# All queries and keys of a latent-attention layer made one stage earlier, stored to DRAM and loaded back; the gate rows made one stage later

## The chip, the cores and the metric

The kernel runs on one core of one Trainium2 chip. A core has a matrix engine (PE, with its weight loads shown apart as PEld), a vector engine (DVE), a scalar engine (ACT), a general engine (POOL) and a queue engine (SP) that here only starts transfers. On-chip operands lie in a memory of 128 partitions; matrix products land in PSUM, eight banks of 128x512 floats. The metric is the device time in microseconds (us); what is compared is the median of several executions, and lower is better.

## The reference

One layer of a diffusion backbone over 1024 latent tokens (`NL`) and 128 context tokens, 1152 in all (`NT`), with D = 1024. What matters here is the attention branch and the gates:

```
h      = rms_norm(x) * (1 + scale) + shift          # shift, scale, gate from silu(cond) @ w_ada
u_f, z_f, cq, ckv, k_rope, z_a, g_f, g_a = split(h @ w_in)
q      = rms_norm(cq, q_norm_g) @ w_uq               # 8 heads x (64 + 32 rotary)
k, v   = split(rms_norm(ckv, kv_norm_g) @ w_ukv)     # 8 heads x 64 each, plus 32 shared rotary key columns
attn   = softmax((q k^T + q_r k_r^T) / sqrt(96)) v   # latent queries see context cache + latent keys
y_f    = (fourier_mix(u_f) * silu(z_f)) @ w_f_out
y_a    = (attn * silu(z_a)) @ w_a_out
y      = rms_norm(x + gate * ((sigmoid(g_f)*y_f + sigmoid(g_a)*y_a) @ w_out), final_norm_g)
```

All products are made at nearly fp32 accuracy: each operand is split into a high and a low part, and `mm3` issues three matmuls (high x high, high x low, low x high) for every product.

## The kernel before

The work runs through stages, each with its own PSUM pool. First the input is normalised, transposed and mixed; then pairs of 128-column blocks of the input projection are made (`pair`, until about 427 us). After that come three stages that the change touches.

**The Fourier output map** (about 427 to 497 us, the loop `for m in range(8)` at L1027). For each of eight 128-channel blocks m and three chunks c of 384 tokens, twelve matmuls (four k-blocks of `mm3`) make a chunk; DVE multiplies it with the gate path `gfl` (L1044), and the row block `mf` is stored to DRAM. At the head of each m the weights and `gfl` of m+1 are loaded (`load_half`, `load_gf`, queued on SP). Between the chunks other work is woven in: `low_tr` transposes the low-rank rows of ten token tiles and splits them into `cqh/cql` (query latent), `kvh/kvl` (key-value latent) and the rotary rows 64 to 127 of the key tiles `KB` (latents) and `KC` (context); `load_gate`, `ada_rows` and `gate_row` make the 2x1024 gate row at m = 1 to 4; `k_up` makes the keys of heads 0 and 1 at m = 5; `q_chunk` makes one query chunk (head 0, tokens 0 to 383) at m = 7; `value_map` makes the values, seven of ten tiles here or just behind.

**Attention** (about 497 to 777 us). Eight heads run one after another. The order of their steps is written out by hand in `HSEQ` (heads 0 to 6) and `LSEQ` (head 7): `s` is a score chunk (`mm3` into PSUM and a DVE minimum, L1099), `m` the minimum over chunks, `e` the exponential on ACT (L1110), `T` a transpose of probabilities on PE (L1131) with its split by ACT (L1132) and DVE (`lo_dve`, L109), `V` the product with the values (L1151, L1152). In the same order stand `L` (load the next head's query weights and, for odd heads, the next pair's key weights), `Q` (three per head: chunks 1 and 2 of this head's queries and chunk 0 of the next head's, `q_chunk`) and `K` (`k_up`, one matmul group for a pair of heads, its copy on ACT at L981 and its splits on POOL; in even heads only the second half's splits, `k_split`). `P` in head 7 loads ahead for the merge stage.

**The merge** (about 777 to 840 us). For each m, `merge_part` makes the attention output map, gates it, adds `mf` and splits the sum into `mh/ml`; `load_out` loads and splits a part of the last weight matrix. `merge_open(m)` starts the loads of m + `AHEAD` (3). The last stage reads the gate row from `gate_d`.

The tiles named `U(...)` all come out of one pool of 43 equal buffers (`NU`), H tiles out of another of four. A planner places the instructions on each engine's queue by their priority in program order and by its own estimate of when their inputs and a free buffer are there; an engine then works through its queue strictly in that order, and SP does so too with its transfers.

Of the kernel before, what the change touches and what calls it, by code (L numbers as in the profile page):

```python
# [59 lines left out]
VS = (3, 0, 0)  # L60


@with_exitstack
def kernel(ctx: ExitStack, tc: tile.TileContext, a: dict):
# [376 lines left out]
    def split_w(src, shape):  # L441
        raw = U(shape, F32, "wr")
        nc.sync.dma_start(raw, src)
        return split(raw)
# [7 lines left out]
    low_d = dram.tile([9, P, 448], F32, name="low_d")  # L452
# [54 lines left out]
    def low_out(c, pss):  # L507
# [8 lines left out]
        for j, ps in enumerate(pss):  # L516
            t = 3 * c + j
            row = H([P, 448], s="low")
            xk = ps[:, 384:416].rearrange("p (a b i) -> p a b i", a=2, b=2)
            if t < 8:  # L520
# [6 lines left out]
                for r in range(2):  # L527
                    dve.tensor_tensor(out=row[:, 384 + 32 * r : 416 + 32 * r], in0=t2.rearrange("p a b i -> p (a b i)"),
                                      in1=t1.rearrange("p a b i -> p (a b i)"), op=ALU.add)
            else:  # L530
                for r in range(2):
# [318 lines left out]
    def low_load(i):  # L850

        rows = U([P, 2, 448], s="low")
        for e in range(2):
# [3 lines left out]
            else:  # L857
                nc.sync.dma_start(row[:, 256:384], a["cache_ckv"])
                nc.sync.dma_start(row[:, 384:416], a["cache_krope"])
                nc.sync.dma_start(row[:, 416:448], a["cache_krope"])  # L860
# [26 lines left out]

    for i, (kind, dst, blk, m) in enumerate(PAIRS):
# [12 lines left out]

    gate_d = dram.tile([2, D], F32, name="gate_d")
    grow = [U([2, D], F32, "grow") for _ in range(2)]
    nc.sync.dma_start(grow[1], a["b_gate"].to_broadcast([2, D]))

    def load_gate(j):
        parts = []
        for q in range(4):
            w = U([P, 2, 512], s="wgate")
            nc.sync.dma_start(w, a["w_gate"][j, q])  # L910
            parts.append(w)
        return parts

    def gate_row(rows, j):
        ps = MM()
        pe.matmul(ps[0:2, :], sel, rows, start=True, stop=True)
        sl = slice(j * 512, (j + 1) * 512)
        dve.tensor_tensor(out=grow[0][:, sl], in0=ps[0:2, :], in1=grow[1][:, sl], op=ALU.add)
        if j == 1:
            nc.sync.dma_start(gate_d, grow[0])  # L920

# [11 lines left out]
    def put_kv(ckvn, krd, kv_h, kv_l, kb, sl, gain=True):  # L933
# [3 lines left out]
        pe.transpose(pt[0:64, 128:256], krd, ident)  # L937
# [5 lines left out]
        for h, l in kb:  # L943
            act.copy(h[64:128, sl], pt[0:64, 128:256])
            dve.tensor_tensor(out=l[64:128, sl], in0=pt[0:64, 128:256], in1=h[64:128, sl].bitcast(F32), op=ALU.subtract)

    def low_tr(t, row):
        sl = slice(t * P, (t + 1) * P)
        ckn, kd = row[:, 256:384], row[:, 384:448]
        if t == 9:  # L950
            put_kv(ckn, kd, kvh[:, 1024:1152], kvl[:, 1024:1152], KB, slice(1024, 1152), False)
            return
        if t < 8:
            put_kv(ckn, kd, kvh[:, sl], kvl[:, sl], KB, sl)
        else:
            put_kv(ckn, kd, kch, kcl, KC, slice(0, 128))
# [14 lines left out]
    def k_up(wk, c, kf):  # L971
# [5 lines left out]
        mm3(ps[:, 0:n], wk[:, 0, :], wk[:, 1, :], rh, rl, True, True)  # L977
        for e in range(2):
            x = H([64, CH], s="kf") if e == 0 else None
            x = x[:, 0:n] if e == 0 else (kf[0][:, sl] if c < 3 else kf[1])  # L980
            act.copy(x, ps[64 * e : 64 * e + 64, 0:n])  # L981
            if e == 0:
                k_split(0, c, x)

    def k_split(e, c, x):
        if c < 3:
            sl = slice(c * CH, (c + 1) * CH)
            kh, kl = KB[e][0][0:64, sl], KB[e][1][0:64, sl]
        else:
            kh, kl = KC[e][0][0:64, :], KC[e][1][0:64, :]  # L990
        hi_pool(kh, x)
# [517 lines left out]
```

## Time and profile before

| | |
|---|---|
| Median of 3 runs (lowest to highest) | 937.79 us (937.47 to 938.55) |
| The profiled execution's own time | 938.17 us |
| Its span in the trace | 936.4 us |
| Mean granted PE clock | 0.989 |
| HBM read and written | 81.74 MB and 32.83 MB |
| Chain that ended last, share of PE | 76% |

The span runs from the first to the last instruction of the trace; the profiled execution's time is 1.8 us longer. A matmul's record lasts until its result is written, while the next one starts before that, so that busy time on PE is not a count of work: the distance between the starts of two matmuls is what one costs when they follow each other without a gap. A weight load (PEld) runs under the matmul before it; where PEld sits idle, PE's queue waits.

### The profile page before, as it was taken

What the parts mean: (1) busy time and instruction counts of PE and PEld (TensorE: products, weight loads), DVE (VectorE), ACT (ScalarE), POOL (GpSimd) and SP (SyncE); (2) the same over time, 40 slices, a digit from 0 to 9 for tenths busy, and PEclk for the clock granted to TensorE, in tenths of its full rate; (3) what the DMA queues carried; (4) which work ended last, traced back from release to release, by engine and by line L of the source; (5) the groups of instructions that cost most, each with busy time, mean ns of one, the idle gap of its engine ahead of it and who ended that gap; (6) DMA issues with size and microseconds to landing.
All of it is one profiled execution on the core that took longest, in us unless ns stands there. A gap on an engine that the chain in (4) does not pass through costs nothing.

```text
span 936.4 us, 15839 instructions
## 1 busy us (share of the span) xinstructions
PE 892.8 (95%) x5814; PEld 841.9 (90%) x5814; DVE 629.2 (67%) x1276; ACT 422.9 (45%) x1149; POOL 411.9 (44%) x494
## 2 busy tenths in 40 slices
PE   4878999999999999999999999999999999999996
PEld 3667999899999999998899999999999989988885
DVE  3898466655545544658538889889889887784333
ACT  7555374411112211135128787787787782212111
POOL 1586313674444448942051263263263126763221
PEclk9889999999999999999999999999999999999999
DMA  9923645422222244278733000000000147342222
GB/s 365 361 89 120 229 144 188 155 97 96 97 97 96 97 146 146 97 280 295 268 139 135 7 7 4 7 7 4 7 7 2 62 182 280 107 157 90 91 92 88
DMA packets 35797, 115.59 MB, mean 123 GB/s; under 512 B 4484, under 2 KB 9348, under 8 KB 35720
## 3 DMA queue, kind: packets, MB, share of 16 engines
q1 hardware_dynamic: 31688, 105.94, 31.5%
q10 hardware_dynamic: 3168, 6.16, 1.8%
q0 software_dynamic: 864, 2.49, 0.8%
q8 instruction: 46, 0.75, 0.3%
q14 instruction: 31, 0.25, 0.1%
HBM read 81.74 MB, written 32.83 MB: 122 GB/s over the span
## 4 chain that ended last, share of the span: by engine, by line
PE 76%; POOL 4%; DVE 3%; DMA 1%; ACT 1%; issue 1%; DVEq 0%; SPq 0%; ACTq 0%; POOLq 0%
PE mm L122 21%; PE mm L126 20%; PE mm L125 20%; PE mm L1131 6%; PE mm L1152 4%; PE mm L1151 3%; POOL z L761 1%; POOL z L765 1%; DMA fz_d<-z 1%; DVE tl L109 1%; POOL wp L106 1%; DMA wr<-in_w_f_out 1%; POOL mfl L1295 1%; DVE hTl L109 0%; PE mm L1186 0%
## 5 line engine op out<-in xcount | busy, mean ns | idle before, releaser
L1099 DVE TENSOR_REDUCE s<-mm 128x1 f32<-128x384 f32 (+1 forms) x200 | 104.8, 540 | 15.6 <-PE mm L126 13.8
L109 DVE TENSOR_TENSOR tl<-mm,th 128x384 fp32r<-128x384 f32 (+1 forms) x216 | 102.9, 504 | 16.8 <-ACT th L1132 16.2
L1110 ACT ACTIVATE p<-mm,s 128x384 f32<-128x384 f32 x192 | 110.2, 588 | 7.3 <-DVE s L1104 7.1
L122 PE MATMUL mm<-hTh,wp 128*128 128x288 f32 x352 | 104.4, 297 | 0.0
L125 PE MATMUL mm<-hTl,wp 128*128 128x288 f32 x352 | 104.4, 297 | 0.0
L126 PE MATMUL mm<-hTh,wp 128*128 128x288 f32 x352 | 104.3, 297 | 0.0
L1132 ACT CAST th<-mm 128x384 fp32r<-128x384 f32 (+1 forms) x216 | 89.4, 461 | 25.6 <-PE mm L1131 22.7
L1131 PE MATMUL mm<-c,p 128*128 128x128 f32 x576 | 95.7, 274 | 1.9 <-ACT s L981 0.5
L1131 PEld LDWEIGHTS mm<-c,p 128*128 128x128 f32 x576 | 71.7, 140 | 9.0 <-DVE tl L109 1.8
L122 PE MATMUL mm<-th,wp 128*128 128x288 f32 x264 | 78.4, 297 | 1.3 <-ACT th L559 0.6
L125 PE MATMUL mm<-tl,wp 128*128 128x288 f32 x264 | 78.1, 296 | 1.5 <-DVE tl L109 1.5
L126 PE MATMUL mm<-th,wp 128*128 128x288 f32 x264 | 78.1, 296 | 0.0
L1152 PE MATMUL mm<-tl,v 128*128 128x384 f32 (+1 forms) x216 | 74.0, 346 | 0.2 <-DVE tl L109 0.2
L1151 PE MATMUL mm<-th,v 128*128 128x384 f32 (+1 forms) x216 | 73.2, 343 | 0.0
L122 PE MATMUL mm<-kh,q 128*128 128x384 f32 x192 | 70.7, 368 | 0.4 <-DVE tl L109 0.3
L122 PEld LDWEIGHTS mm<-hTh,wp 128*128 128x128 f32 x352 | 67.0, 190 | 0.3 <-ACT u L792 0.3
L125 PEld LDWEIGHTS mm<-hTl,wp 128*128 128x128 f32 x352 | 66.8, 190 | 0.0
L126 PEld LDWEIGHTS mm<-hTh,wp 128*128 128x128 f32 x352 | 66.8, 190 | 0.0
L125 PE MATMUL mm<-kl,q 128*128 128x384 f32 x192 | 64.7, 337 | 0.0
L126 PE MATMUL mm<-kh,q 128*128 128x384 f32 x192 | 64.0, 338 | 0.0
L106 POOL TENSOR_SCALAR q<-qf 128x384 fp32r<-128x384 f32 x24 | 12.3, 512 | 104.1 <-DVE qf L1004 65.4
L122 PE MATMUL mm<-hi,mh 128*128 128x512 f32 (+1 forms) x152 | 57.7, 383 | 0.0
(343 smaller groups left out, 2580.8 us busy)
## 6 DMA issues: line engine op xcount, KB each, us to landing
wr<-in_w_in SPq DMA_DIRECT2D x24, 512.0 KB, 4.2
x<-in_x_sample SPq DMA_DIRECT2D x16, 512.0 KB, 4.8
wada<-in_w_ada SPq DMA_DIRECT2D x16, 512.0 KB, 10.2
h_d<-hf SPq DMA_DIRECT2D x8, 576.0 KB, 3.3
gf_d<-z SPq DMA_DIRECT2D x8, 576.0 KB, 4.7
gfl<-gf_d SPq DMA_DIRECT2D x8, 576.0 KB, 4.6
mf_d<-mf SPq DMA_DIRECT2D x8, 576.0 KB, 3.2
gal<-ga_d SPq DMA_DIRECT2D x8, 576.0 KB, 3.7
```

What stands on the lines that cost most here:

```text
L106: pool.tensor_scalar(out=out, in0=x, scalar1=1.0, scalar2=1.0, op0=ALU.mult, op1=ALU.mult)
L109: dve.tensor_tensor(out=out, in0=x, in1=hi.bitcast(F32), op=ALU.subtract)
L122: i = pe.matmul(out, lh, rh, start=start, stop=False, skip_group_check=on)
L125: pe.matmul(out, lh, rl, start=False, stop=False, skip_group_check=on)
L126: pe.matmul(out, ll, rh, start=False, stop=stop, skip_group_check=on)
L761: pool.tensor_tensor(out=out, in0=out, in1=tmp, op=ALU.mult)
L1099: dve.tensor_reduce(out=self.nb if self.last else self.mx[:, kc : kc + 1], in_=ps[:, 0:n], axis=AX.X, op=ALU.min)
L1110: act.activation(self.p[:, kc * CH : kc * CH + n], self.ps[kc][:, 0:n], AF.Exp, scale=-1.0, bias=self.nb, accum_out=SSP[(self.h // 2) % 2] ...
L1131: pe.transpose(pt[:, j * P : (j + 1) * P], self.pr[j][:, kt * P : (kt + 1) * P], ident)
L1132: act.copy(th[:, i, 0:n], pt[:, 0:n])
L1151: pe.matmul(po[:, 0:n], V[kt][:, h, :], th[:, i, 0:n], start=(self.nv == 0), stop=False)
L1152: pe.matmul(po[:, 0:n], V[kt][:, h, :], tl[:, i, 0:n], start=False, stop=(self.nv == 8))
```

## The change

All 24 query chunks (8 heads x 3) and all 16 key groups (4 pairs of heads x 4 chunks) are made inside the Fourier output map, and each is stored to DRAM (`q_d`, `k_d`). A list `TASKS` says what stands behind each of the 24 chunks of that map (`L` low_tr, `W` and `w` weights, `k`, `q`, `v` value map, `K` the load of head 0's keys, `Q` the load of a query chunk of head 0). In attention, `L` becomes the load of the next head's keys into `KB`/`KC` (four transfers into partitions 0 to 63), `Q` the load of a query chunk one or two chunks ahead, and `K` does nothing. The orders `HSEQ` and `LSEQ` stay as they are. The high part of a query is copied by ACT instead of POOL; keys are split by ACT and DVE straight from PSUM for both heads of a pair at once. The rotary key columns are written four times instead of twice into a low-rank row (512 wide instead of 448), so that their transpose lands on partitions 64 to 127 by itself. The gate row's loads, matmuls and store move into the merge.

```diff
+TASKS = (
+    "L0 L1", "L2 L3 W", "L4 L5 W", "L6 L7", "L8 L9 W", "k00 k01", "k02 k03 q00", "q01 q02 W", "k10 k11 k12", "k13 q10 q11 W", "q12 q20",
+    "q21 q22", "k20 k21 k22", "k23 q30 q31", "q32 q40", "q41 q42", "k30 k31 k32 w", "k33 q50 q51", "q52 q60", "q61 q62", "q70 q71 K Q0",
+    "q72 v Q1", "v v", "v v", "v v",
+)
...
-            row = H([P, 448], s="low")
+            row = H([P, 512], s="low")
...
-                for r in range(2):
+                for r in range(4):
                     dve.tensor_tensor(out=row[:, 384 + 32 * r : 416 + 32 * r], in0=t2.rearrange("p a b i -> p (a b i)"),
...
+    def up_weights():
+        if not wk:
+            wk.extend(split_w(a["w_uk"].rearrange("h p c -> p h c"), [P, 4, P], lo_pool))
+        else:
+            p = len(wq)
+            wq.append(split_w(a["w_uq"][2 * p : 2 * p + 2].rearrange("h p c -> p h c"), [P, 2, 256], lo_pool))
...
+    q_d = dram.tile([NH, 3, P, 2, CH], F32, name="q_d")
+    k_d = dram.tile([4, P, 2, NT + P], F32, name="k_d")
...
-    def k_up(wk, c, kf):
+    def k_up(p, c):
...
-        mm3(ps[:, 0:n], wk[:, 0, :], wk[:, 1, :], rh, rl, True, True)
-        for e in range(2):
-            x = H([64, CH], s="kf") if e == 0 else None
-            x = x[:, 0:n] if e == 0 else (kf[0][:, sl] if c < 3 else kf[1])
-            act.copy(x, ps[64 * e : 64 * e + 64, 0:n])
-            if e == 0:
-                k_split(0, c, x)
...
+        mm3(ps[:, 0:n], wk[0][:, p, :], wk[1][:, p, :], rh, rl, True, True)
+        k = U([P, 2, CH], F32R, "k")
+        act.copy(k[:, 0, 0:n], ps[:, 0:n])
+        lo_dve(k[:, 1, 0:n], ps[:, 0:n], k[:, 0, 0:n])
+        nc.sync.dma_start(k_d[p][:, :, sl], k.bitcast(F32)[:, :, 0:n])
+
+    def k_load(h):
+        rows = slice(64 * (h % 2), 64 * (h % 2) + 64)
+        src = k_d[h // 2][rows]
+        for (kh, kl), sl in ((KB[h % 2], slice(0, NT)), (KC[h % 2], slice(NT, NT + P))):
+            nc.sync.dma_start(kh[0:64, :].bitcast(F32), src[:, 0, sl])
+            nc.sync.dma_start(kl[0:64, :].bitcast(F32), src[:, 1, sl])
+
+    def q_up(h, c):
...
         q = U([P, 2, CH], F32R, "q")
-        hi_pool(q[:, 0, :], qf)
+        act.copy(q[:, 0, :], qf)
         lo_pool(q[:, 1, :], qf, q[:, 0, :])
-        return q
+        nc.sync.dma_start(q_d[h, c], q.bitcast(F32))
+
+    def q_load(h, c):
+        t = U([P, 2, CH], F32R, "qt")
+        nc.sync.dma_start(t.bitcast(F32), q_d[h, c])
+        return t
...
     for m in range(8):
-        if m in (1, 3):
-            wgt = load_gate(m // 2)
-        elif m in (2, 4):
-            rows = ada_rows(wgt, 2, 512, MM())
...
+            for k in TASKS[3 * m + c].split():
+                task(k)
...
             elif o == "L":
                 if h + 1 < NH:
-                    if h % 2:
-                        wk, kf = load_split(a["w_uk"][h // 2 + 1], P), new_kf()
-                    wq1 = load_split(a["w_uq"][h + 1], 256)
+                    k_load(h + 1)
...
             elif o == "Q":
                 nq += 1
-                if nq < 3:
-                    qs[nq] = q_chunk(wq, nq)
+                if nq == 1:
+                    qs[2] = q_load(h, 2)
                 elif h + 1 < NH:
-                    q0 = q_chunk(wq1, 0)
+                    qn[nq - 2] = q_load(h + 1, nq - 2)
...
+    wgt, rows = [load_gate(0), load_gate(1)], []
     merge_open(0)
     merge_open(1)
...
     for m in range(2, 8):
         merge_open(m)
+        if m > 2 and rows:
+            gate_row(rows.pop(0), m - 3)
+        if wgt:
+            rows.append(ada_rows(wgt.pop(0), 2, 512, MM()))
         for c in range(3):
             merge_part(m, c)
```

More of the change, by code (lines that the diff above doesn't have):

```diff
@@ L450, in load_r @@
         return t
-    low_d = dram.tile([9, P, 448], F32, name="low_d")
+    low_d = dram.tile([9, P, 512], F32, name="low_d")
     f_d = dram.tile([4, P, NT], F32, name="f_d")
@@ L530, in low_out @@
             else:
-                for r in range(2):
+                for r in range(4):
                     act.copy(row[:, 384 + 32 * r : 416 + 32 * r], ps[:, 384:416])
@@ L850, in low_load @@
     def low_load(i):
-        rows = U([P, 2, 448], s="low")
+        rows = U([P, 2, 512], s="low")
         for e in range(2):
@@ L858, in low_load @@
                 nc.sync.dma_start(row[:, 256:384], a["cache_ckv"])
-                nc.sync.dma_start(row[:, 384:416], a["cache_krope"])
-                nc.sync.dma_start(row[:, 416:448], a["cache_krope"])
+                for r in range(4):
+                    nc.sync.dma_start(row[:, 384 + 32 * r : 416 + 32 * r], a["cache_krope"])
         return rows
@@ L898 @@
         pair(b, nb_, kind, dst, m, fs, {} if nb_ else {0: fz_load, 1: low_loads, 7: gf_first, 5: fz_split})
[L902 to L920, printed above, removed]
     cqh = [U([P, NT], F32R, "cqh") for _ in range(2)]
@@ L943, in put_kv @@
         for h, l in kb:
-            act.copy(h[64:128, sl], pt[0:64, 128:256])
-            dve.tensor_tensor(out=l[64:128, sl], in0=pt[0:64, 128:256], in1=h[64:128, sl].bitcast(F32), op=ALU.subtract)
+            act.copy(h[64:128, sl], pt[64:128, 128:256])
+            lo_dve(l[64:128, sl], pt[64:128, 128:256], h[64:128, sl])
     def low_tr(t, row):
         sl = slice(t * P, (t + 1) * P)
-        ckn, kd = row[:, 256:384], row[:, 384:448]
+        ckn, kd = row[:, 256:384], row[:, 384:512]
+        if t == 8:
+            put_kv(ckn, kd, kch, kcl, KC, slice(0, 128))
+        else:
+            ks = sl if t < 8 else slice(1024, 1152)
+            put_kv(ckn, kd, kvh[:, ks], kvl[:, ks], KB, ks, t < 8)
         if t == 9:
-            put_kv(ckn, kd, kvh[:, 1024:1152], kvl[:, 1024:1152], KB, slice(1024, 1152), False)
             return
[L953 to L956, printed above, removed]
         pt = MM()
@@ L1068 @@
         za.append(z)
-    for _ in range(3):
-        value_map(len(V))
+    for k in TASKS[24].split():
+        task(k)
     stage.close()
@@ L1220 @@
             osb = U([P, NT], F32, "osb")
-        nk = nq = npre = 0
-        q0 = None
+        nq = npre = 0
+        qn = {}
         for part in LSEQ if h == NH - 1 else HSEQ:
@@ L1297, in merge_part, with load_gate, gate_row @@
         lo_dve(ml[m][:, sl], mf[:, sl], mh[m][:, sl])
+    gate_d = dram.tile([2, D], F32, name="gate_d")
+    grow = [U([2, D], F32, "grow") for _ in range(2)]
+    nc.sync.dma_start(grow[1], a["b_gate"].to_broadcast([2, D]))
+    def load_gate(j):
+        parts = []
+        for q in range(4):
+            w = U([P, 2, 512], s="wgate")
+            nc.sync.dma_start(w, a["w_gate"][j, q])
+            parts.append(w)
+        return parts
+    def gate_row(rows, j):
+        ps = MM()
+        pe.matmul(ps[0:2, :], sel, rows, start=True, stop=True)
+        sl = slice(j * 512, (j + 1) * 512)
+        dve.tensor_tensor(out=grow[0][:, sl], in0=ps[0:2, :], in1=grow[1][:, sl], op=ALU.add)
+        if j == 1:
+            nc.sync.dma_start(gate_d, grow[0])
     def merge_open(m):
```

76 lines of the change are left out of this document (28 added, 48 removed).

## The prediction

> **What bounds the kernel now.** I read the page's first part, then the busy times of chosen stretches (columns: stretch, length, then busy us with the number of instructions for PE, PEld, DVE, ACT, POOL; granted clock; DMA share; GB/s).
>
> ```profile
> span 936.4 us, 15839 instructions
> PE 892.8 (95%) x5814; PEld 841.9 (90%) x5814; DVE 629.2 (67%) x1276; ACT 422.9 (45%) x1149; POOL 411.9 (44%) x494
> 427.00:496.50 69.50, 69.08 (x394) 61.13 (x393) 41.32 (x94) 24.59 (x70) 18.86 (x28) 1.00 0.64 233
> 496.50:566.60 70.10, 69.77 (x457) 67.39 (x456) 60.05 (x144) 55.78 (x171) 27.25 (x45) 1.00 0.09 32
> 566.60:636.60 70.00, 69.69 (x468) 67.36 (x467) 60.40 (x147) 55.34 (x173) 29.40 (x50) 1.00 0.02 6
> 636.60:706.60 70.00, 69.69 (x467) 67.36 (x466) 60.40 (x147) 55.26 (x172) 29.38 (x50) 1.00 0.02 6
> 706.60:777.00 70.40, 67.75 (x458) 64.08 (x457) 62.28 (x153) 54.29 (x166) 18.29 (x33) 1.00 0.30 104
> 777.00:840.00 63.00, 62.18 (x339) 59.73 (x339) 51.27 (x62) 12.25 (x24) 45.45 (x40) 1.00 0.51 172
> ```
>
> The first stretch is the Fourier output map, the next four are the pairs of heads, the last is the merge. PE bounds all three stages: it is busy over 98% of each but the last pair of heads (96%), at full clock. Busy matmuls overlap, so I check the pace by the starts of matmuls that follow without a gap. From the order of time on PE, the first and the last of 40 matmuls of 384 columns in a row, and three pieces of the chain that ended last:
>
> ```profile
> 165.68 0.34 PE L126 MATMUL mm<-hTh,lo 128*128 128x384 f32 x1
> ...
> 172.54 0.34 PE L126 MATMUL mm<-hTh,lo 128*128 128x384 f32 x1
> 457.83 1.85 PE mm L231 x16
> 464.10 0.95 PE mm L916 x2
> 508.20 0.66 PE mm L1131 x6
> ```
>
> 39 steps in 6.86 us: 0.176 us for each 384-column matmul. A 128-column one costs 0.66/6 = 0.11. So PE has work without a gap almost everywhere, and moving PE work from one stage to another gains nothing by itself: only places where PE waits can be won, and any new wait is paid in full.
>
> **The change part by part.** *Moved PE work.* A query chunk is 2 x 3 matmuls of 384 columns, 6 x 0.176 = 1.06 us. 23 of 24 chunks leave attention (one is made in the map already). A pair's keys are 9 such matmuls and 3 of 128 columns, 1.58 + 0.33 = 1.9 us; three of four pairs leave. Attention loses 23 x 1.06 + 3 x 1.9 = 30.1 us of PE work, the map gains 30.1. The gate's two groups of 16 matmuls and two of 2 (rows above: 1.85 and 0.95) are 2 x (1.85 + 0.95) = 5.6 us that leave the map and are added to the merge. Sum over the stages: 0. The transposes of rotary keys get wider weights, but stay 128-column matmuls: 0.
>
> *Waits that go.* In attention PE waits once per pair, where the pair's keys are made:
>
> ```profile
> 626.60:631.60 5.00, 4.69 (x30) 3.82 (x29) 3.43 (x9) 4.97 (x16) 5.00 (x9) 1.00 0.10 30
> PEld mm L1131 <- ACT s L981: 1.2, 3, 0.4
> 556.27 0.26 ACT L981 COPY kf<-mm 64x128 f32<-64x128 f32 x1 [1.91 <-PE mm L126]
> ```
>
> ACT stands 1.91 us at the copy of the last key chunk, since that copy is ahead of the probability splits on its queue; PE then waits for those. In the second pair's five microseconds weight loads are idle 5.00 - 3.82 = 1.18 us, and the row of the waits says three times. I take 3 x 1.2 = 3.6 us as gone. What is late next there is DVE (below). In the map, PE waits for the gate's transfers and for weights queued on SP behind them:
>
> ```profile
> PEld mm L122 <- POOL whl L106: 1.3, 1, 1.3
> PEld mm L231 <- DMA wgate<-in_w_gate: 0.9, 2, 0.6
> 436.82 5.44 DMA wr<-in_w_f_out
> ```
>
> 1.3 + 0.9 = 2.2 us gone. Together -5.8 us.
>
> *DVE in attention, the cover that shrinks.* Rows of DVE and ACT, the query's and key's own work, and two stretches inside the second pair of heads:
>
> ```profile
> L1004 DVE TENSOR_TENSOR qf<-mm,tab 128x384 f32<-128x384 f32 x24 | 13.2, 552 | 2.1 <-PE mm L126 1.2 <-PE mm L1131 0.4 <-issue 0.3
> L981 ACT COPY kf<-mm 64x384 f32<-64x384 f32 x24 | 11.4, 477 | 13.3 <-PE mm L126 13.0
> L112 POOL TENSOR_TENSOR q<-qf,q 128x384 fp32r<-128x384 f32 x24 | 24.3, 1013 | 1.5
> 576.60:581.60 5.00, 5.00 (x37) 4.91 (x36) 5.00 (x13) 4.33 (x13) 1.90 (x3) 1.00 0.04 13
> 606.60:611.60 5.00, 5.00 (x35) 4.89 (x35) 5.00 (x14) 4.61 (x15) 2.48 (x6) 1.00 0.02 3
> ```
>
> Of PE a pair loses 6 x 1.06 + 1.9 + the wait of 1.2 = 9.5 of 70.0 us; DVE loses only 6 x 0.552 = 3.3 of 60.4 (the key splits are on POOL). So PE would need 60.5 us, DVE 57.1: its share rises from 86% to 94%. ACT loses 6 x 0.477 and some, to 52 of 60.5. Already now DVE has stretches of five microseconds without a gap. Bounds: below, 0, since PE keeps its pace in just those two rows; above, DVE holds no higher share than its present 60.40/70.00, a pair then lasts 57.1/0.863 = 66.2, that is 5.7 more for each of four pairs, 23 us. The nearest rows are the two stretches, near the low end; I take one new DVE wait per pair of the size of the ACT wait that it replaces, 4 x 1.2 = +4.8 us. POOL's query splits (24 x 1.01 us) leave attention, but PE waits for POOL nowhere there: 0.
>
> *The map: transfers, buffers, SP's order.* Stores of 24 x 0.393 MB of queries and 5.24 MB of keys are added here. While they are made (from `k00` to `q72` of the task list: 17 chunks x 12 matmuls x 0.176 = 35.9, 24 query chunks 25.4, four key pairs 7.6; 68.9 us), the stage also stores six `mf` and loads five `gfl` (11 x 0.59 MB), five `w_f_out` blocks, two query weights and the value weight (8 x 0.262 MB), and for attention one set of keys and one query chunk (1.05 MB): in all 24.3 MB, 353 GB/s. The page has the rate of each 23.4 us slice:
>
> ```profile
> GB/s 365 361 89 120 229 144 188 155 97 96 97 97 96 97 146 146 97 280 295 268 139 135 7 7 4 7 7 4 7 7 2 62 182 280 107 157 90 91 92 88
> ```
>
> At its best, 365, the 24.3 MB take 66.6 of 68.9 us: hidden, but with 3% to spare. The Trainium skill ("DMA: Bandwidth & Descriptors", section Where 436 GB/s comes from) puts the limit between HBM and one core at about 358 GB/s, which speaks against this change; an estimate by that page is 67.9 us, 1.3 more, still under PE's time. The first slice's 365 lies above the page's figure, so the measurement decides.
>
> New waits: SP's store of a query waits for POOL's low part (1.01 us) behind ACT's copy, and behind it on SP stand the next m's weights and `gfl`; ACT's copy into the query tile waits for one of 43 buffers, and the splits of keys and values stand behind it on ACT. Counted from the code, 36 buffers are taken at m = 3 (8 fz, 4 cq, 2 kv, 4 key tiles, tab, 10 weights, 7 of the map itself), which leaves 7 for tiles on their way out. Bounds: 0, since loads run one m (12 us) ahead; above, the wait for `whl` of 1.3 us in each of six m, 8 us. I take two of them, +2.6 us. Elsewhere the map has cover: ACT 24.59 and DVE 41.32 of 69.50, and 40 copies of 0.477 and 40 DVE operations of 0.552 come into a stage that grows by 22 us net.
>
> *Merge.* 4.2 MB of gate weights are loaded while 43 buffers are short (attention's own end holds many, and the row from SP's order of time shows loads of `w_out` that wait already):
>
> ```profile
> 807.15 23.66 SPq L443 DMA_DIRECT2D wr<-in_w_out x4
> wgate<-in_w_gate SPq DMA_DIRECT2D x8, 512.0 KB, 5.7
> ```
>
> Freed in turn are the query and key latents and the table (7 buffers), so head 7's loads can start sooner. Bounds 0 to 4.4 (the gate's waits as in the map, 2.2, for each of its two halves); I take 1.
>
> *Low rows.* 16 more DVE operations and two on ACT:
>
> ```profile
> L528 DVE TENSOR_TENSOR low<-s,s 128x32 f32<-128x32 f32 x16 | 3.3, 246 | 0.2
> low<-low_d SPq DMA_DIRECT2D x9, 224.0 KB, 7.1
> ```
>
> 16 x 0.246 = 3.9 us at most on a DVE with gaps there, and 0.3 MB more to store and load. If that cover is gone, the last tiles' four operations cost 1 us; I take 0.3.
>
> *Key and query loads in attention.* 0.66 MB and three query chunks a head, against 6 GB/s now, issued a third of a head or more ahead: 0. No row shows a transfer into 64 partitions; at twice the time per byte it would still be hidden.
>
> *Sum*, against the profiled execution's own 938.17 (span 936.4 and 1.8 around it): -5.8 + 4.8 + 2.6 + 1.0 + 0.3 = +2.9, 941.1; the median of the runs lies 0.4 lower, so **940.7**.
>
> **The rivals.** *PE alone stays the bound (faster).* Place: attention. All waits that go are won and DVE follows at 94%; then 937.8 - 5.8 + 1 to 3 of small change = 933 to 935. For it: PE's pace in the two stretches with a DVE without a gap. Against it: the hand-written order was laid out with `Q` and `K` in it, each of which gave DVE about half a microsecond to catch up. It decides from there on that DVE's new waits stay under 3.9 us in all.
>
> *A wash.* DVE and the map cost about half of what I take: 936 to 939.6.
>
> *The map becomes bound by transfers and buffers.* Loads stand behind stores at 97% of the best rate, and PE waits in most m: the 8 us of the upper bound instead of 2.6, or a rate that holds only at 297 to 339 GB/s, as in this stage's stretches now:
>
> ```profile
> 420.00:425.00 5.00, 5.00 (x38) 5.00 (x37) 5.00 (x9) 2.56 (x7) 2.61 (x3) 1.00 0.94 339
> 440.00:465.00 25.00, 24.57 (x143) 19.00 (x137) 15.50 (x39) 7.26 (x23) 2.69 (x5) 1.00 0.80 297
> ```
>
> 24.3 MB at 339 are 71.7 us (+2.2), at 297 81.8 (+12.3): 943 to 953. Against it: at 0.80 share the second row isn't full.
>
> *It doesn't do what it says*: attention doesn't get shorter, because DVE bounds it at its present share: the upper bound above, up to 959. A full DVE beside a full PE speaks against it.
>
> **How the numbers follow.** Forecast (DVE and queues give back more than is won, 939.7 to 944): 0.36. PE alone: 0.27. Wash: 0.24. Transfers or DVE bound (944 to 959): 0.13. The range 932.8 to 948.5 leaves out little below (all waits won and more) and the upper part of the last case. A measurement here tells about 0.2% (1.9 us) from no change; faster 0.27, within it 0.24, slower 0.49.
>
> **What would show it.** Attention ends about 250 us after it starts, now 280; the map lasts about 92, now 69.5; the merge about 69, now 63. In the waits of attention, "ACT s L981" is gone, and weight loads wait for DVE's splits and PSUM instead, in four places or more. In the map, DMA share is over 0.9 and POOL's `whl` waits for its load. I am wrong if attention's PE is idle less than 4 us more than its work (then faster), or if PE waits over 5 us in the map (then 945 and up).

## The result and the profile after

The changed kernel takes **953.12 us** (median of 4 runs, 951.75 to 954.83) against 937.63 for the kernel before in the same measurement (4 runs, 936.87 to 938.55): a ratio of 1.0166, 95% interval 1.0146 to 1.0185, so 15.5 us slower. The forecast was 940.7 with a range of 932.8 to 948.5: the direction was right, the size was not.

The page of the profiled execution (952.68 us), first part: PE's busy time is 4.0 us longer than before, POOL's 56.5 us shorter, and the span is 14.2 us longer. So the 14 us are mostly time in which PE has nothing to do.

```profile
span 950.6 us, 16026 instructions
PE 896.8 (94%) x5814; PEld 838.1 (88%) x5814; DVE 635.3 (67%) x1307; ACT 426.5 (45%) x1159; POOL 355.4 (37%) x393
GB/s 365 363 75 137 224 168 227 74 115 120 119 103 111 128 67 125 162 315 194 329 377 370 68 53 78 78 9 71 78 79 20 136 162 340 171 149 101 89 89 89
```

Where it came from is read from PE's matmuls in order of time: the last matmul of the pair loop (`acc` pairs, the front's end), the first score, and the first matmul of the merge. "Forecast" is the sum of the prediction's terms for that stretch.

| stretch | before, us | after, us | change | forecast |
| --- | --- | --- | --- | --- |
| start to the end of the pair loop | 424.1 | 418.0 | -6.1 | +0.3 (low rows) |
| from there to the first score (map) | 71.9 | 101.1 | +29.2 | +24.9 (30.1 - 5.6 - 2.2 + 2.6) |
| first score to the merge (attention) | 280.7 | 264.2 | -16.5 | -28.9 (-30.1 - 3.6 + 4.8) |
| merge and output, to the end | 159.7 | 167.3 | +7.6 | +6.6 (5.6 + 1.0) |
| span | 936.4 | 950.6 | +14.2 | +2.9 |

Attention is short of the forecast by 12.4 us, the map by 4.3, the merge by 1.0; the front gave back 6.4 that nobody had counted. The stages as busy times of chosen stretches, after (columns as above: stretch, length, then busy us with instructions for PE, PEld, DVE, ACT, POOL; granted clock; DMA share; GB/s): the map, the four pairs of heads, the merge, and attention as a whole.

```profile
418.00:519.00 101.00, 97.05 (x547) 93.75 (x546) 63.62 (x134) 38.32 (x100) 43.57 (x46) 0.98 0.89 311
519.00:584.00 65.00, 61.92 (x400) 57.72 (x398) 55.17 (x135) 51.08 (x157) 3.20 (x8) 1.00 0.29 96
584.00:649.00 65.00, 62.82 (x417) 58.96 (x417) 56.69 (x141) 51.81 (x162) 7.07 (x15) 1.00 0.20 58
649.00:714.00 65.00, 62.81 (x417) 58.95 (x417) 56.81 (x141) 51.81 (x162) 7.08 (x15) 1.00 0.20 58
714.00:783.30 69.30, 65.60 (x436) 59.80 (x437) 59.91 (x148) 55.02 (x169) 10.03 (x21) 1.00 0.30 104
783.30:841.50 58.20, 56.72 (x328) 51.60 (x327) 42.94 (x57) 11.21 (x22) 37.80 (x35) 1.00 0.61 226
519.10:783.30 264.20, 253.05 (x1669) 235.37 (x1668) 228.59 (x562) 209.62 (x650) 27.38 (x59) 1.00 0.25 79
```

Attention of the kernel before, in the same view:

```profile
496.00:776.70 280.70, 277.10 (x1843) 266.35 (x1841) 243.32 (x589) 221.06 (x675) 104.02 (x175) 1.00 0.11 37
```

Two things are to be seen. DVE was busy 243.32 of 280.70 us before, 86.7%, and is busy 228.59 of 264.20 after, 86.5%: its share has not risen at all. And PE has 174 matmuls fewer, while weight loads, whose busy time overlaps least, are idle 28.8 us instead of 14.4. A pair in the middle has lost 50 matmuls of its 467 and only 5.0 us of its 70.0; the matmuls alone are 8.3 (6 x 1.06 + 1.9).

The waits of weight loads in attention (us in total, times, longest). The one row for the keys, "ACT s L981", is gone as forecast. In its place stand many short waits, more of them for ACT's probabilities and sums (L1105; 11.6 us in all rows of the view) than for DVE (6.3 us). The four largest:

```profile
PEld mm L1146 <- ACT s L1105: 3.6, 7, 0.7
PEld mm L1126 <- DVE osb L1160: 3.2, 5, 0.9
PEld mm L1126 <- ACT p L1105: 2.8, 9, 0.8
PEld mm L129 <- ACT p L1105: 2.3, 2, 1.9
```

The groups of the page show the ring behind them. Each row ends with the engine's idle time ahead of it and what ended it: DVE's minimum waits for PE's scores, ACT's exponential for DVE's minimum (L1099 after, L1104 before), DVE's split of the transposed probabilities for ACT's copy (L1127 after, L1132 before). First before, then after:

```profile
L1099 DVE TENSOR_REDUCE s<-mm 128x1 f32<-128x384 f32 (+1 forms) x200 | 104.8, 540 | 15.6 <-PE mm L126 13.8
L1110 ACT ACTIVATE p<-mm,s 128x384 f32<-128x384 f32 x192 | 110.2, 588 | 7.3 <-DVE s L1104 7.1
L109 DVE TENSOR_TENSOR tl<-mm,th 128x384 fp32r<-128x384 f32 (+1 forms) x216 | 102.9, 504 | 16.8 <-ACT th L1132 16.2
L1094 DVE TENSOR_REDUCE s<-mm 128x1 f32<-128x384 f32 (+1 forms) x200 | 105.2, 541 | 19.6 <-PE mm L133 17.8
L1105 ACT ACTIVATE p<-mm,s 128x384 f32<-128x384 f32 x192 | 110.2, 592 | 9.3 <-DVE s L1099 9.2
L116 DVE TENSOR_TENSOR tl<-mm,th 128x384 fp32r<-128x384 f32 (+1 forms) x216 | 101.9, 504 | 12.2 <-ACT th L1127 11.3
```

The engines waited for each other in this way before the change too, and for about as long (39.7 us in the three rows, 41.1 after). New is that PE, with less work of its own, now waits for the ring. The chain that ended last, taken from the first score to the merge, before and after (the view cuts its line off at the end):

```profile
by line: PE mm L1131 21.5%; PE mm L122 16.2%; PE mm L126 15.7%; PE mm L125 15.5%; PE mm L1152 11.8%; PE mm L1151 11.5%; DVE tl L109 1.5%; PE mm L1186 1.4%; ACT th L1132 0.9%; DVE s L1099 0.9%; ACT p L1110 0.6%; issue 0.5%; DVE osb L1165 0.4
by line: PE mm L1126 16.3%; PE mm L1146 11.9%; ACT p L1105 10.8%; PE mm L1147 9.8%; PE mm L129 9.5%; PE mm L133 8.9%; PE mm L132 8.9%; DVE tl L116 4.9%; DVE s L1094 4.8%; ACT th L1127 4.7%; issue 2.6%; DVE osb L1160 1.2%; ACT s L1105 1.1%;
```

Before, ACT and DVE hold some 4% of that chain, after some 27%: the path through attention now runs through both.

The map after its start, and the start itself:

```profile
430.00:515.00 85.00, 84.45 (x486) 82.81 (x486) 49.96 (x103) 29.01 (x73) 38.63 (x41) 1.00 0.92 323
423.00:426.40 3.40, 1.18 (x7) 0.46 (x5) 3.21 (x9) 1.85 (x7) 0.17 (x1) 0.99 0.99 344
426.50:429.70 3.20, 2.87 (x9) 2.90 (x10) 3.04 (x12) 2.96 (x12) 1.47 (x2) 0.50 0.11 32
```

From 430 to 515 PE is busy 84.45 of 85.00 us with the DMA share at 0.92: the transfers are hidden. The loss is at the start. The task list packs ten low-row transposes (`L0` to `L9`) into five chunks, their copies and splits pile up on DVE (busy 3.21 of 3.40 us) and PE waits; then the granted clock is 0.50 for 3.2 us. The two waits there:

```profile
PEld mm L957 <- DVE mf L1052: 1.3, 1, 1.3
PEld mm L934 <- DVE mf L1052: 1.2, 1, 1.2
```

### The profile page after: what moved, and what is told of

The parts are those of the page before. It is cut to its first block, busy times and chain, and to the rows that moved or that the text cites. A ratio compares the mean times of both kernels' runs of the same rounds, so it can differ in the third digit from the quotient of the medians.

```text
span 950.6 us, 16026 instructions
## 1 busy us (share of the span) xinstructions
PE 896.8 (94%) x5814; PEld 838.1 (88%) x5814; DVE 635.3 (67%) x1307; ACT 426.5 (45%) x1159; POOL 355.4 (37%) x393
## 4 chain that ended last, share of the span: by engine, by line
PE 62%; DVE 7%; ACT 6%; POOL 6%; issue 3%; DMA 3%; SPq 1%; DVEq 0%; POOLq 0%; ACTq 0%
PE mm L129 17%; PE mm L133 17%; PE mm L132 17%; PE mm L1126 5%; PE mm L1146 3%; ACT p L1105 3%; PE mm L1147 3%; DVE tl L116 1%; DVE s L1094 1%; ACT th L1127 1%; POOL z L768 1%; POOL mfl L1279 1%; POOL z L772 1%; DVE lo L116 1%; DMA fz_d<-z 1%
## 5 line engine op out<-in xcount | busy, mean ns | idle before, releaser
L1105 ACT ACTIVATE p<-mm,s 128x384 f32<-128x384 f32 x192 | 110.2, 592 | 9.3 <-DVE s L1099 9.2
L116 DVE TENSOR_TENSOR tl<-mm,th 128x384 fp32r<-128x384 f32 (+1 forms) x216 | 101.9, 504 | 12.2 <-ACT th L1127 11.3
L1127 ACT CAST th<-mm 128x384 fp32r<-128x384 f32 (+1 forms) x216 | 89.1, 463 | 24.3 <-PE mm L1126 22.0
L1126 PE MATMUL mm<-c,p 128*128 128x128 f32 x576 | 92.4, 275 | 3.0 <-DVE osb L1160 1.9
L113 POOL TENSOR_SCALAR s<-s 128x128 f32<-128x128 f32 x36 | 10.2, 298 | 191.0 <-DVE s L1175 166.5
L1126 PEld LDWEIGHTS mm<-c,p 128*128 128x128 f32 x576 | 69.3, 140 | 11.9 <-DVE osb L1160 3.2
L129 PE MATMUL mm<-kh,qt 128*128 128x384 f32 x192 | 69.8, 364 | 3.4 <-ACT p L1105 1.8
L129 PEld LDWEIGHTS mm<-hTh,wp 128*128 128x128 f32 x352 | 66.2, 188 | 0.0
L132 PEld LDWEIGHTS mm<-hTl,wp 128*128 128x128 f32 x352 | 66.2, 188 | 0.0
L133 PEld LDWEIGHTS mm<-hTh,wp 128*128 128x128 f32 x352 | 66.2, 188 | 0.0
L133 PE MATMUL mm<-kh,qt 128*128 128x384 f32 x192 | 64.8, 337 | 0.0
L132 PE MATMUL mm<-kl,qt 128*128 128x384 f32 x192 | 64.7, 337 | 0.0
L133 PE MATMUL mm<-hi,ml 128*128 128x512 f32 (+1 forms) x152 | 58.1, 383 | 0.7 <-DVE ml L116 0.7
```

The lines of the kernel that those rows point to most:

```text
L113: pool.tensor_scalar(out=out, in0=x, scalar1=1.0, scalar2=1.0, op0=ALU.mult, op1=ALU.mult)
L116: dve.tensor_tensor(out=out, in0=x, in1=hi.bitcast(F32), op=ALU.subtract)
L129: i = pe.matmul(out, lh, rh, start=start, stop=False, skip_group_check=on)
L132: pe.matmul(out, lh, rl, start=False, stop=False, skip_group_check=on)
L133: pe.matmul(out, ll, rh, start=False, stop=stop, skip_group_check=on)
L1105: act.activation(self.p[:, kc * CH : kc * CH + n], self.ps[kc][:, 0:n], AF.Exp, scale=-1.0, bias=self.nb, accum_out=SSP[(self.h // 2) % 2] ...
```

## The experiments

Theory A: the loss is in attention, whose pairs have a floor of some 65 us that DVE and ACT set together, since score, minimum, exponential, transpose and split wait for each other in turn; PE work taken out below that floor is not won, while the map pays for all of it. Rivals: the map's stores and loads; the crowded start of the map; the gate rows in the merge; the hand-written order, which was laid out with the queries and keys in it. Unless a kernel is said to be built on before, it is built on after. Ratios are to the kernel before, measured beside it.

**Is PE still the bound in attention?** `e2_filler` puts back the queries' PE work alone, as 23 times six matmuls that nothing reads:

```diff
             elif o == "Q":
                 nq += 1
+                if nq < 3 or h + 1 < NH:
+                    fp, (fh, fl), fq = MM(), KB[h % 2], qs[0]
+                    for k in range(2):
+                        mm3(fp[:, :CH], fq[:, 0, k * P : (k + 1) * P], fq[:, 1, k * P : (k + 1) * P], fh[:, 0:CH], fl[:, 0:CH], k == 0, k == 1)
```

> Changed kernel with six matmuls of 384 columns put back at each of the 23 places where a query chunk stood in attention (23 x 1.06 = 24.4 us of PE work), on tiles that are there, into a PSUM bank that nothing reads: no work for DVE, ACT or POOL. Theory 'PE is no longer the bound in attention': much of it goes into PE's new waits; attention (first score to first matmul of the merge, 264 us in the changed kernel) grows by 8 to 14 us, total 961 to 967. Rival 'PE is the bound there': it grows by 24, total about 977.

Measured: 961.59 us, ratio 1.0271 (1.0246 to 1.0297). Attention in the view of stretches:

```profile
519.10:792.50 273.40, 269.56 (x1808) 260.26 (x1806) 230.06 (x562) 213.04 (x650) 27.49 (x59) 1.00 0.24 77
```

24.4 us of PE work cost 9.2 us (273.4 against 264.2), within the 8 to 14 of the theory; 15 us vanished in waits that were there anyway.

`e9_floor` goes the other way and takes out work: the products of the values with the low parts of the probabilities are left out, DVE and ACT keep everything.

```diff
-            pe.matmul(po[:, 0:n], V[kt][:, h, :], th[:, i, 0:n], start=(self.nv == 0), stop=False)
-            pe.matmul(po[:, 0:n], V[kt][:, h, :], tl[:, i, 0:n], start=False, stop=(self.nv == 8))
+            pe.matmul(po[:, 0:n], V[kt][:, h, :], th[:, i, 0:n], start=(self.nv == 0), stop=(self.nv == 8))
```

> The kernel after without the products of the values with the probabilities' low parts (54 matmuls of 384 columns a pair, 9.5 us of PE; DVE and ACT keep all their work). Theory (DVE and ACT set a pair's length, 57 and 52 us of work in a chain): attention, 264 us in the kernel after, stays at 250 or more, and PE idles some 14 us a pair. Rival (a pair is PE's work plus 5 us of waits, whatever the work): attention 226 to 232.

Measured: 951.69 us (two runs), ratio 1.0172 (1.0146 to 1.0198). Attention, and its second pair:

```profile
584.50:648.50 64.00, 58.13 (x361) 51.74 (x361) 54.85 (x139) 52.06 (x162) 7.07 (x15) 0.97 0.21 59
519.80:781.60 261.80, 233.80 (x1454) 206.41 (x1452) 226.95 (x563) 209.61 (x650) 27.69 (x60) 0.98 0.26 81
```

216 matmuls are gone. The expectation took all of them at 384 columns, 38 us; the trace has 144 of 384 columns and 72 of 256, and with starts 0.176 and about 0.12 us apart that is some 34 us of PE. Attention got 2.4 us shorter, and weight loads idle 55 us in it. That is the floor: below some 65 us a pair PE's work hardly matters. The granted clock fell to half three times in this attention (last section), 3.2 us and a little more each, which costs at most half of that, some 5 us; so the floor at full clock may lie a little lower.

**What makes the floor?** `e3_dve` leaves out the minimum over the third key chunk (the scores are scaled by 0.01 so that the exponentials stay finite), `e4_act` the accumulator reads of the exponentials (the sums are set to one), `e13_both` both. The first edit below is that of `e3_dve`, the second that of `e4_act`.

```diff
-            dve.tensor_reduce(out=self.nb if self.last else self.mx[:, kc : kc + 1], in_=ps[:, 0:n], axis=AX.X, op=ALU.min)
+            if self.last or kc < 2:
+                dve.tensor_reduce(out=self.nb if self.last else self.mx[:, kc : kc + 1], in_=ps[:, 0:n], axis=AX.X, op=ALU.min)
...
-            act.activation(self.p[:, kc * CH : kc * CH + n], self.ps[kc][:, 0:n], AF.Exp, scale=-1.0, bias=self.nb,
-                           accum_out=SSP[(self.h // 2) % 2][:, self.h % 2, self.t, kc : kc + 1])
+            act.activation(self.p[:, kc * CH : kc * CH + n], self.ps[kc][:, 0:n], AF.Exp, scale=-1.0, bias=self.nb)
```

> Changed kernel without the minimum over the third key chunk of each latent score row (64 of 192 reductions on DVE, 64 x 0.54 = 35 us of DVE work in attention); the scores are scaled by 1/100 so that the exponentials stay finite. PE, ACT and the transfers are the same. Theory 'DVE bounds attention': attention goes from 264 to 246-250, near PE's own work of about 240, total 935 to 940. Rival 'ACT bounds it, or the order of the steps does': attention loses under 5, total 948 to 953.

> Changed kernel without the row sums of the exponentials (the 200 accumulator reads on ACT, 0.21 us each, 40 us of ACT work in attention); the sums are set to one instead. Theory 'DVE bounds attention': it loses under 5 of 264 us, total 948 to 953. Rival 'ACT bounds it': attention goes to 246-250, total 935 to 940. If both this and the DVE run shorten it by 8 or more, it is the chain through both (score, minimum, exponential, release of the bank) that PE waits for, not one engine's load.

> The kernel after with both reliefs of e3 and e4 at once: no minimum over the third key chunk (scores scaled by 0.01) and no accumulator reads (sums set to one). Theory (DVE and ACT hold attention, each alone keeps the other's share): attention falls to 240 to 247 us, PE's own work of some 60 us a pair, 929 to 935 in all. Rival (a third thing holds it, the number of PSUM banks or the written order): attention stays at 250 or more, 939 and up.

Measured: 941.87 (ratio 1.0055, 1.0036 to 1.0074), 942.98 (1.0065, 1.0044 to 1.0085) and 936.99 us (1.0001, 0.9983 to 1.0019). Attention in the three, first DVE relieved:

```profile
520.10:773.30 253.20, 248.55 (x1670) 235.95 (x1668) 201.29 (x498) 210.51 (x650) 27.55 (x59) 1.00 0.26 82
```

ACT relieved:

```profile
519.60:773.60 254.00, 248.33 (x1670) 235.35 (x1668) 226.72 (x556) 194.28 (x451) 27.48 (x58) 1.00 0.26 83
```

Both:

```profile
520.90:768.30 247.40, 244.56 (x1669) 235.97 (x1668) 198.81 (x490) 193.99 (x450) 26.97 (x57) 1.00 0.26 84
```

Neither "DVE alone" (246 to 250 us of attention in `e3_dve`) nor "ACT alone" (the same in `e4_act`) came true. DVE's busy time falls by 27.3 us in the first (228.59 to 201.29), ACT's by 15.3 in the second (209.62 to 194.28). Either relief shortens attention by 10 to 11 us, though DVE was at only 87% of it and ACT at 79%; both together by 16.8, and PE is then busy 244.56 of 247.40. With both relieved, ACT and DVE hold only some 4% of the chain that ended last in attention. So it is the chain through both engines, not one of them full, and once both are relieved nothing else of size is left. What the runs do not tell apart is the engines' work and the time for which it holds the eight PSUM banks: a relief shortens both, and the use of the banks was not varied by itself. (For `e13_both` the stretch came out 0.4 us and the total 2.0 us above the upper end of what was expected.)

**Does the written order hold it?** `e11_lag` lets the products follow three transposes behind instead of two: `LAG, TOFF = 2, 9` becomes `LAG, TOFF = 3, 9`.

> The kernel after with the products three transposes behind instead of two (LAG 3), no work changed. If the hand-written order, laid out with the queries and keys in it, is too tight for the splits, attention loses 4 us or more: 944 to 949. Theory (DVE's and ACT's work sets the pair): within 2 us of the kernel after, 951 to 955.

Measured: 949.25 us, ratio 1.0146 (1.013 to 1.0161); attention 261.1 us, which lies between the two forecasts. 3 of the 17 us that attention gave back may be the order's. The interval overlaps that of the kernel after, so this is not settled, and no order was written anew.

**The crowded start of the map.** `e1_spread` has one low-row transpose to a chunk and the later tasks moved back to fit: the list begins `"L0", "L1 W", "L2", "L3 W", "L4 k00", "L5", "L6 k01 W"`.

> Changed kernel with another task list: one transpose task (L) behind each chunk of the Fourier output map instead of two, the key and query tasks shifted to make room; the same tasks otherwise. Theory 'pile-up': PE stands 4.5 us at the map's start because ten transpose tasks in five chunks are more work for ACT and DVE than PE gives them time for, and the clock is halved for 3.4 us after it: the map gets 4 to 5 us shorter, total about 948.5. Rival 'the list is not what matters, transfers and buffers fill the map': the stall moves or stays, total 952 to 955.

Measured: 950.22 us, ratio 1.0142 (1.0121 to 1.0164). The stretch to the first score is 97.8 us instead of 101.1 and has no stretch at half clock; new waits of 2.2 us for the key latent (ACT kvh) and 1.5 us for the query latent (ACT cqh) took back part of it. So the crowding cost about 3 us; that rests on the stretches of the two traces, since the intervals of the two ratios overlap (1.0121 to 1.0164, and 1.0146 to 1.0185 for the kernel after).

**The front.** `e6_hoist` is the kernel before with head 0's key and query weights loaded through a `U` buffer instead of an `H` buffer, `e7_rows` the kernel before with the wide low rows (four copies of the rotary key, `put_kv` at full width), and `e8_gate` the kernel before with the gate rows in the merge as in the change's own diff. The first edit below is that of `e6_hoist` (`load_u` is `load_split` with its raw tile from `U`), the second the core of `e7_rows`.

```diff
-            wk, wq = load_split(a["w_uk"][0], P), load_split(a["w_uq"][0], 256)
+            wk, wq = load_u(a["w_uk"][0], P), load_u(a["w_uq"][0], 256)
...
-            row = H([P, 448], s="low")
+            row = H([P, 512], s="low")
-                for r in range(2):
+                for r in range(4):
```

> The kernel before, but head 0's key and query weights are loaded through U buffers, so that the planner leaves their two transfers beside the map and not ahead of combine(3)'s on SP. Theory: the two transfers held SP, and PE lost 4 us and half a clock behind it; pairs end near 418 instead of 424, in all 931 to 933. Rival (the front's 6 us come from the wider low rows): 937 to 938.5.

> The kernel before with the low rows 512 wide and the rotary key four times in each, and put_kv's transpose at full width, alone. Theory (the front's gain comes from the SP order): the two weight transfers still stand ahead of combine(3) and the time stays, 937 to 939. Rival (the low rows shift the front): pairs end near 418, 931 to 933.

> The kernel before with the gate rows made in the merge stage, alone. Theory by the kernel after's merge (+7.7 for 5.6 of PE) and the map's 5.6 and two waits of 2.2: 936.5 to 938.5, no difference that counts. Rival (the gate's place is a good part of the loss of 15): 941 or more.

Measured: 932.83 us, ratio 0.9969 (0.9953 to 0.9985); 935.93, ratio 0.9999 (0.9983 to 1.0015); 936.3, ratio 1.0004 (0.9988 to 1.0021). In the kernel before, SP's order of time has two weight loads, which attention's first head needs 300 us later, in front of the two loads of the last `combine`. They stand there because their `H` buffers look free to the planner, and SP waits for POOL and for a store before it gets past them:

```profile
155.24 0.33 SPq L965 DMA_DIRECT2D hw<-in_w_uk  x1
162.50 0.33 SPq L965 DMA_DIRECT2D hw<-in_w_uq  x1
162.92 0.38 SPq L551 DMA_DIRECT2D xa<-h_d  x1
163.35 0.42 SPq L552 DMA_DIRECT2D xb<-h_d  x1
```

Without them the two loads go out almost five microseconds sooner (`e6_hoist`, same view):

```profile
158.16 0.33 SPq L551 DMA_DIRECT2D xa<-h_d  x1
158.59 0.37 SPq L552 DMA_DIRECT2D xb<-h_d  x1
```

PE from 175 to 185 us, before:

```profile
175.00:185.00 10.00, 7.92 (x46) 7.45 (x46) 9.87 (x13) 1.75 (x3) 5.59 (x6) 0.83 0.38 138
```

and in `e6_hoist`, where it starts 78 matmuls instead of 46:

```profile
175.00:185.00 10.00, 10.00 (x78) 10.00 (x77) 8.32 (x12) 2.10 (x5) 4.81 (x5) 1.00 0.31 108
```

The change removes these two loads with `load_split`, so it won the stall by accident. Its worth over many runs is 2.9 us, not the 5 to 6 I expected: the stall is there in the profiles of before, `e7_rows` and `e8_gate`, but in the last it stays short and without half clock. The low rows cost nothing that can be measured, and neither does the gate's place by itself: `e8_gate` lost in the merge and output (161.4 us to the last output matmul, 152.1 before) what it won in the map (65.1 us to the first score, 71.9 before) and in attention (278.9, 280.7 before).

**Keys or queries?** `e5_keys` moves only the keys; queries are made in attention by `q_chunk` as before, with one low-row transpose to a chunk. `e10_best` also writes the first pair's keys straight into attention's tiles, in `k_up`:

```diff
+        if p == 0:
+            for e in range(2):
+                kh, kl = (x[0:64, sl] if c < 3 else x[0:64, :] for x in (KB[e] if c < 3 else KC[e]))
+                act.copy(kh, ps[64 * e : 64 * e + 64, 0:n])
+                lo_dve(kl, ps[64 * e : 64 * e + 64, 0:n], kh)
+            return
```

> The kernel after, but queries stay in attention as before (each chunk made there, head 0's first one in the map); only the keys are made in the map, stored and loaded, with one low_tr per chunk. Chain theory (attention is set by the chain of score, minimum, exponential and bank release on DVE and ACT): DVE has its 60 us a pair again, so attention keeps most of its length, 272 to 277 us of 280.7 before, and the gain is the ACT copies of the keys; the map is near 78 us, the front 6 shorter than before: 930 to 936 in all. Rival (the stored tiles and their transfers cost the time): a map over 85 us and a total above 938.

> The kernel of e5 with the first pair's keys written straight into attention's key tiles, so that no load of keys stands on SP ahead of the map's weights. Theory (moving the keys pays, moving the queries doesn't): front near 418.5, map 71, attention 270, merge and output 160, in all 927 to 931, against 935 to 938 of before. Rival (moving anything into the map costs what it wins): 935 or more.

Measured: 940.36 us, ratio 1.005 (1.0032 to 1.0067), and 935.01, ratio 0.9995 (0.9983 to 1.0006). Both miss their forecasts; `e10_best` came out at its rival's number. Attention did what was forecast or better (269.7 us in both), but the map did not: 81.6 and 79.7 us instead of 78 and 71. The traces name a fault of mine: SP is one queue. In `e10_best` stores of keys, which wait for DVE's low part (L114), stand ahead of the next weights of the map, and SP is at the three stores of the first of these rows for 7 us:

```profile
450.35 7.28 SPq L983 DMA_DIRECT2D k_d<-k  x3
457.73 0.56 SPq L448 DMA_DIRECT2D wr<-in_w_uv  x1
...
461.17 0.45 SPq L844 DMA_DIRECT2D wr<-in_w_f_out  x1
```

PE then waits for the split of those weights:

```profile
PEld mm L127 <- POOL whl L111: 6.6, 1, 6.6
```

`e12_actq` issues these stores from ACT (`nc.scalar.dma_start(k_d[p]...)`), and the two last kernels also load the value weights and head 0's query weights later: `e14_gmap` with the gate rows in the map as before, `e14_gmerge` with them in the merge.

> The kernel of e10 with the stores of the keys issued by ACT instead of SP, so that no weight of the map stands behind a store that waits for DVE. Theory (the map's stall in e5 and e10 is that queue): the 8 us at 462 to 470 are gone, map 71, in all 925 to 930. Rival (the stall is a lack of buffers or of DMA rate, or it moves to ACT's queue): 933 or more.

> The kernel of e12 with the value weights and head 0's query weights loaded two and six thirds of an m later, and the gate rows back in the map as before. Theory: the 2 us at 462 are gone, the map is near 78 us with the gate in it, attention 270, merge and output 151; in all 926 to 930. Rival (keys in the map win nothing over the kernel before without its hoisted loads): 932 or more.

> The same with the gate rows in the merge, as in e12. Theory (the gate's place costs a merge 3.7 us over its work and wins a map 2): 1 to 3 us more than e14_gmap. Rival: no difference.

Measured: `e12_actq` 936.05 us (ratio 0.9994, 0.9977 to 1.0011). In its profiled execution the wait of 6.6 us is down to 2.2, which is left where POOL splits head 0's query weights ahead of the map's, and the map lasts 73.4 us instead of 79.7. But that execution took 932.16 us, the least of its twelve, which go up to 938.49, and the median is no lower than that of `e10_best`: the rival's number came true, and what the other executions waited for no trace shows. So moving the stores off SP won nothing that could be measured by itself; the gain came only with the later weights. `e14_gmap` **929.83** (0.9932, 0.9911 to 0.9953) and `e14_gmerge` 931.13 (0.9938, 0.9917 to 0.996): the intervals lie on each other, so the gate's place makes no difference that could be measured. Both beat the kernel before and the changed one. Half of that is the front's (`e6_hoist`, 0.9969, whose interval touches or overlaps both), so the totals alone do not show that moving the keys gains. `e8_gate` has the gate rows in the same place as `e14_gmerge` and all keys but the first pair's made in attention; beside it `e14_gmerge` has a map 6.5 us longer (71.6, 65.1) and an attention 9.2 us shorter (269.7, 278.9). `e14_gmerge`, its map from the end of the pair loop to the first score, then attention:

```profile
420.10:491.70 71.60, 71.21 (x410) 68.20 (x409) 49.33 (x114) 28.02 (x80) 13.38 (x18) 1.00 0.68 242
491.70:761.50 269.80, 268.21 (x1808) 260.40 (x1807) 239.95 (x586) 211.57 (x650) 70.20 (x119) 1.00 0.17 50
```

The same two stretches of `e1_spread`, which differs from it above all in that the queries are made in the map too:

```profile
418.50:516.30 97.80, 94.64 (x547) 92.28 (x547) 61.28 (x134) 38.54 (x100) 43.44 (x46) 1.00 0.90 317
516.30:780.60 264.30, 253.14 (x1670) 235.37 (x1668) 228.76 (x563) 210.03 (x650) 27.56 (x59) 1.00 0.25 81
```

That pair of rows holds the result. The queries' 24.4 us of matmuls lengthen the map by 26.2 us and shorten attention by 5.5. The ratios say the same: 1.0142 - 0.9938 = 0.0204, 19 us. What the change cost, in ratios to before: keys, front and gate -0.0062, queries +0.0204, the crowded start 1.0166 - 1.0142 = +0.0024; together +0.0166. (The two kernels also differ in the engine that issues the keys' stores, in the first pair's keys and in when the value weights come; what that is worth is in the queries' part of this sum. Taken from `e5_keys`, which stores and loads all keys by SP as `e1_spread` does, the queries' part is only 1.0142 - 1.005 = 0.0092, 9 us, but in that kernel's map PE waits 10 us for `whl`. So 19 us is their price against a map without such waits.)

## Why the prediction was wrong, point by point

*Moved PE work, 30.1 and 5.6 us, sum 0.* The sizes were right: in the pair of rows above, 24.4 us of matmuls lengthen a map by 26.2. But "sum 0" takes for granted that PE's work is what attention costs, and below 65 us a pair it is not (`e9_floor`).

*Waits that go, 5.8 us.* The mechanism was right for the keys: "ACT s L981" is gone from attention. The size was read wrongly: the row "1.2, 3, 0.4" says 1.2 us in total over three waits, not three times 1.2, and the 1.18 us of idle weight loads in the stretch beside it are of any cause. That the 3.6 was not too much is luck: a kernel that moves only the keys (`e14_gmerge`) has an attention of 269.8 us for 280.7, and of these 10.9 us only 5.7 are PE work. In the map, the two rows of the gate and of `whl` are gone as well.

**DVE in attention, +4.8: the step that failed.** Removed were 30.1 + 3.6 = 33.7 us and won 16.5, so the term measured 17.2 and not 4.8. The work itself was sized well: a pair in the middle has 56.7 us of DVE and 51.8 of ACT, forecast 57.1 and 52. I had put its upper bound at 23, from a DVE that holds its share of 86%, and had then taken the low end because two stretches of five microseconds showed DVE without a gap. Those stretches show that DVE can be full for 5 us when it has a backlog; they say nothing of a whole pair, in which DVE waits for PE's scores and for ACT's copies. The row of a whole pair was the nearest row, and it gave the upper bound: 66.2 us a pair, against 65.0 measured in the middle two. The text also called the cause DVE alone, and named waits for DVE's splits as the sign; weight loads wait more for ACT (11.6 us) than for DVE (6.3), and `e3_dve` and `e4_act` show that ACT's work counts as much. What stands in the place of "one new DVE wait per pair" is the ring of score, minimum, exponential, copy and split, which held a pair at about 65 us as it is written. ACT's share rose only from 78.8 to 79.3%, which is why no row of busy time showed it.

*The map, +2.6.* The stretch came out 4.3 over the forecast, so the term measured 6.9, but not by the transfers, buffers and SP order that I priced: from 430 on PE is busy 84.45 of 85.00 us. The largest part is the crowded start, which I had costed at nothing: the ten transposes were counted as work moved within a stage with cover, 24.59 us of ACT and 41.32 of DVE in 69.50, a mean over the stage, where the cover is asked for in its first 20 us. `e1_spread` puts it at 3 us; what the rest is stays open. My SP mechanism is to be seen in another kernel, the profiled `e10_best`, where PE waits 6.6 us behind it; what it is worth over many runs is not shown, since `e12_actq` was no faster.

*Merge, +1.0 (0 to 4.4).* 2.0 measured beyond the 5.6 of work. One wait holds most of it, a matmul of the gate row behind ACT's copy of the `ada` rows, which, by the trace, itself stood until DVE had split a weight (`whl`, L116):

```profile
PEld mm L1298 <- ACT ada L247: 1.8, 1, 1.8
```

*Low rows, +0.3.* `e7_rows`: nothing measurable. *Loads of keys and queries in attention, 0*: right, no wait of PE in attention ends with a transfer.

*The front, not in the sum.* The prediction looked at what the change adds to that stage and not at what else the removed `load_split` calls did there. SP's order of time before, shown above, has the two loads at 155 and 162 us. That gain was luck, and it hid part of the loss: without it the changed kernel would have been slower still, by some 3 us going by `e6_hoist`.

*The rivals.* The one that came nearest is "it doesn't do what it says": attention bounded at DVE's present share, up to 959. Attention did get shorter, but DVE's share stayed where it was. It had a part of 0.13, together with the transfers. Against it I wrote that a full DVE beside a full PE speaks against it; that was the same misreading of the two stretches.

## What to carry to other kernels

An engine at 86% of a stage may already be at its limit if it takes turns with others: price the loss of cover by its share over a whole period of the loop, not by the best few microseconds. Before moving PE work out of a stage, ask what the stage would last without it; work taken from below the chain's floor is paid in full where it goes. On a queue that runs in order, a store that waits for a result holds every load behind it, and a planner may put a load far ahead of its need into the same queue.

## What the runs showed of the hardware that was not expected

*Half clock after partial idleness.* In three stretches of 3.4 us in which PE had waits, the granted clock afterwards was: 0.50 for 3.2 us after PE had been busy 1.18 of 3.40 us (kernel after, 423.0 to 426.4, shown above, longest gap 1.03 us); 0.50 after 1.38 of 3.40 (before); 1.00 after 2.16 of 3.40 (`e8_gate`). The two of the kernel before:

```profile
177.60:181.00 3.40, 1.38 (x9) 0.91 (x7) 3.40 (x4) 1.75 (x3) 1.53 (x2) 1.00 0.32 101
181.40:184.60 3.20, 3.20 (x16) 3.20 (x15) 3.07 (x7) 0.00 (x0) 1.07 (x2) 0.50 0.49 179
```

and of `e8_gate`:

```profile
176.80:180.20 3.40, 2.16 (x16) 1.93 (x15) 3.40 (x4) 1.34 (x3) 1.12 (x2) 1.00 0.46 146
180.20:183.60 3.40, 3.40 (x28) 3.40 (x27) 3.30 (x7) 0.41 (x1) 1.26 (x2) 1.00 0.45 165
```

The same came in the attention of `e9_floor`, once in each of its first three pairs; the first of them is shown here, the others fell after 1.45 and 1.44 of 3.40:

```profile
550.70:554.10 3.40, 1.47 (x9) 1.12 (x9) 2.43 (x8) 1.75 (x7) 0.00 (x0) 1.00 0.01 3
554.40:557.60 3.20, 3.20 (x12) 3.10 (x12) 1.11 (x2) 2.98 (x11) 0.00 (x0) 0.50 0.00 0
```

So several short waits close together cost twice, once as waits and once as a slow stretch after them. The Trainium skill ("TensorE: Matmul & The Clock Gate", section Why this matters for your kernels) warns of gaps over about 3 us; here no single gap was above 2.0 us. That PE's busy share over a few microseconds decides is what these six stretches suggest (35 to 43% before the five slow ones, 64% before the one that stayed at full clock). It was not tested by itself, and the length of 3.4 us was chosen, not measured.

*DMA rate.* The map after moved 377 GB/s over a whole 23.8 us slice (the row of slices above), more than the 365 that the prediction took for the best rate and than the 358 which the Trainium skill ("DMA: Bandwidth & Descriptors", section Where 436 GB/s comes from) names as the limit between HBM and one core.
